# Another order of the last additions, roots and scalings on VectorE and ScalarE behind the last product of a two-layer trunk

## The chip, the cores and the metric

The kernel runs on one core of a Trainium2 chip. The metric is the device time of one execution, in microseconds (us). The work is split over TensorE (PE, matrix products; PEld, its weight loads), VectorE (DVE), ScalarE (ACT), GpSimd (POOL) and the DMA queues, of which SyncE's (SP) matters here. Each engine carries out its own instructions in a fixed order and waits where an operand or a buffer is not ready.

## The reference, cut to what matters

Two layers over x of 512 rows and 1024 columns, all in float32:

```python
for l in range(DEPTH):                       # DEPTH = 2
    x = x + attention_and_output_projection(rmsnorm(x, attn_norm[l]))
    h = rmsnorm(x, mlp_norm[l])
    u = jnp.square(jax.nn.relu(h @ w_ff1[l]))        # 1024 -> 4096
    x = x + u @ w_ff2[l]                             # 4096 -> 1024
return rmsnorm(x, final_norm)
# rmsnorm(x, g) = x * rsqrt(mean(x * x, axis=-1) + 1e-6) * g
```

The change touches only the last lines: the end of the last `u @ w_ff2[l]`, its addition to x, and the final `rmsnorm`.

## The kernel before, in words

A float32 product is made of three products of rounded parts (`three`, L294 to L299: high by high, high by low, low by high). `W` (class `_Weights`) splits each block of weights into those parts: the high part by ScalarE (L115), the low part by VectorE (L131).

The second MLP product is done in four groups `g`. In each, 2x2 blocks of the operands are combined into seven products, called forms, in the order `FORMS2`: "11", "x3", "21", "x2", "x1", "x4", "22". Their sums are held in PSUM banks: chain X for "11", "x2", "x1"; chain V for "x3", "x4"; chain Y for "21"; Z for the very last form. Every chain has two banks, r = 0 and 1.

The output y lies in SBUF as eight pieces of 128 rows by 512 columns, `place(tb, j)`: row block tb = 0 to 3 and column half j = 0, 1. `gather` (L1076) adds the two banks of a chain, times a per-row factor `r2`, to the pieces (2a, j) and (2a + 1, j): one VectorE instruction each (L1084, out<-in reads y<-X, y<-V, y<-Y or y<-Z). In the last group of the last layer the pieces become whole in this order: (2, 0) and (3, 0) after form "21"; (0, 1) and (1, 1) after "x1"; (0, 0) and (1, 0) after "x4" (the list `came`; bank V0 is finished before V1, L1208); (2, 1) and (3, 1) after "22". For "22" the X banks are gathered first (at L1198, into (2, 1) and (3, 1)), and the product itself is put into new banks: Z0 for all 512 columns of (2, 1), then the first 256 columns of (3, 1) in Z1, then its other 256 columns in a bank called `half` (L1201, L1202). `half` takes over the bank of V0. A product of zeros opens it (L1203), and ScalarE then writes the sum so far of those columns into it (`seed`, L1205), so that the last product ends with the whole value in the bank.

The final norm goes row block by row block:

- `square` (L1107, ScalarE): the sum of squares of one piece, into a column of `fin`. It is two instructions, the square and the read of its accumulator.
- `root` (L1136): VectorE adds the two sums (L1138), GpSimd raises the result to the power -1/2 (L1140).
- `weigh` (L1143, VectorE): one piece times the final gain.
- `store` (L1147): one piece times the root, on ScalarE if the piece was weighed before (L1151), otherwise on VectorE with the gain in the same instruction (L1153), and the piece's DMA to the output.
- `last_row` (L1110): for row block 3, the addition of Z1's 256 columns (L1114, `add`), the squares of the two last parts (L1116, `ends`), the addition of the first three sums (L1119, `part`), that of the last one (L1121, `whole`), and the power (L1122).
- `store_last` (L1125): ScalarE scales (3, 0), VectorE the last two parts of 256 columns (L1130), each with its DMA (L1133).

The order of instructions on an engine is chosen by the framework's scheduler when the kernel is built. `behind(a, b)` adds to that only that a stands behind b, without a wait, and `in_order` (L1158) chains a list of steps in this way. At the end there are two such lists, `first` for VectorE (L1259) and `squares` for ScalarE (L1260).

Of the kernel before, what the change touches and what calls it, by code (L numbers as in the profile page):

```python
# [13 lines left out]
ALU = mybir.AluOpType  # L14
# [149 lines left out]
def trunk(ctx, tc, opened, xT, w, w2, w1, gfin, lamv, cos, sin, out):  # L164
    nc = tc.nc
# [167 lines left out]
    for l in range(L):  # L333
        with ExitStack() as actx:
# [113 lines left out]
            ends = {}  # L448
# [387 lines left out]
        with ExitStack() as fctx:  # L836
# [236 lines left out]
            def place(tb, j):  # L1073
                return y[(tb // 2, j)][:, tb % 2, :]
# [31 lines left out]
            def square(tb, j):  # L1106
                return nc.scalar.activation(  # L1107
                    ft(f"junk{tb}{j}"), place(tb, j), AF.Square, accum_out=fin[:, 4 * tb + 4 + j : 4 * tb + 5 + j])

            def last_row(banks_):  # L1110
                half = [place(3, 1)[:, 0:256], banks_[1][:, 0:256]]
                m = [fin[:, n : n + 1] for n in (16, 17, 18, 19, 0)]
                by = r2[:, 3:4]
                add = nc.vector.scalar_tensor_tensor(  # L1114
                    out=half[0], in0=banks_[0][:, 0:256], scalar=by, in1=half[0], op0=ALU.mult, op1=ALU.add)
                ends = [nc.scalar.activation(  # L1116
                    ft(f"junk3{n}")[:, 0:256], half[n], AF.Square, scale=by if n else 1.0,
                    accum_out=m[4] if n else m[1]) for n in range(2)]
                part = nc.vector.tensor_scalar(  # L1119
                    out=m[2], in0=m[0], scalar1=m[1], scalar2=D * EPS, op0=ALU.add, op1=ALU.add)  # L1120
                whole = nc.vector.tensor_tensor(out=m[4], in0=m[4], in1=m[2], op=ALU.add)  # L1121
                nc.gpsimd.tensor_tensor(out=m[3], in0=m[4], in1=mhalf[:, 0:1], op=ALU.pow)  # L1122
                return add, ends, part, whole

            def store_last(bank_):  # L1125
                o = place(3, 1)
# [31 lines left out]
            def in_order(*steps):  # L1158
                for p, q in zip(steps[1:], steps):
                    behind(p, q)  # L1160
# [7 lines left out]
            for g in range(GROUPS):  # L1168
                end = g == GROUPS - 1
                turn[0] = 0  # L1170
                if g:
                    p_, q_, r_, s_ = r_, s_, p_, q_
                    quad_group(g, 0, (p_, q_, r_))
                    quad_group(g, 1, (s_, r_, q_))
                    rest_of_forms(1, "21")
                else:
                    for k in range(2 * GP):
                        for n, pt in enumerate(block(f"f{l}_{g}_{k}", "any")):
                            if (k, n) == (1, 0):
                                rms_square(ssq, f"m{l}")  # L1180
                        evict_whole(pt, k)
                        h_form(k)
                        if last and k > 3:
                            for tb in (2 * (k % 2), 2 * (k % 2) + 1):
                                forth(tb, 1 - k // 6)
                    p_, q_, r_, s_ = ring[0] % 3, 3, (ring[0] + 1) % 3, (ring[0] + 2) % 3
                    held_on = {"Y": [bank("t", f"Y{l}{r}") for r in range(2)], "V": [bank("mm", f"V{l}{r}") for r in range(2)]}
                chains = {"X": [temp(k, f"X{l}{g}{k}") for k in (p_, q_)], **held_on}
                for form in FORMS2:
                    total, to = SUMS[form], chains[CHAIN[form]]  # L1190
                    opens = form == "11" or g == 0 and form in ("x3", "21")
                    if form == "x4" and not end:
                        to = [temp(k, f"W{l}{g}{k}") for k in (r_, s_)]
                        opens = True
                    work = [(c, i, r, 0) for c in range(GP // 2) for i in range(2) for r in range(2)]
                    tail = end and form == "22"
                    if tail and last:
                        gather(total, to)  # L1198
                        to = [temp(k, f"Z{l}{k}") for k in (r_, s_)]
                        opens = True  # L1200
                        work = [(c, i, r, n) for r, n in ((0, 0), (1, 1), (1, 2)) for c in range(GP // 2) for i in range(2)]  # L1201
                        halves = [to[1], bank("mm", "half")]  # L1202
                        nc.tensor.matmul(  # L1203
                            halves[1][:, 0:256], zeros[:, 0:128], zeros[:, 128:384], start=True, stop=False)
                        seed = nc.scalar.activation(  # L1205
                            halves[1][:, 0:256], place(3, 1)[:, 256:512], AF.Copy, scale=mean[:, 3:4])
                    elif end and last and form == "x4":
                        work.sort(key=lambda e: e[2])  # L1208
                    held = {}
                    for n, (c, i, r, part) in enumerate(work):  # L1210
                        if c not in held:
                            held[c] = W.next("f")
                        u = held[c]
                        hi, lo = (e[:, :, i, :] for e in sides[c])
                        rs = slice(r * P, r * P + P)
                        mine = [m for m, e in enumerate(work) if e[2:] == (r, part)]
                        pt, b_ = to[r], wpair(u, i, 512)
                        if part:
                            pt = halves[part - 1][:, 0:256]
                            b_ = [e[:, 256 * part - 256 : 256 * part] for e in b_]  # L1220
                        three(pt, (hi[:, SIDE[form], rs], lo[:, SIDE[form], rs]), b_,
                              opens and n == mine[0] and part < 2, n == mine[-1], not opens)
                        if tail and last and n == 3:
                            squares.append(square(0, 0))
                            first += [root(0), store(0, 0, False), came[1]]
                            squares += [seed, store(0, 1, True), square(1, 0)]
                            first += [root(1), store(1, 0, False), *gather(total, to, (0,))]
                            squares += [store(1, 1, True), square(2, 1)]
                            first.append(root(2))
                        if end and not last and form == "22" and n % 2:  # L1230
                            h = back(n // 2)
                            rests.append(h[1])
                            halfway = h
                    if tail:
                        break
                    if end or form not in ("x3", "21"):
                        came = gather(total, to)
                    if g and form in ("11", "x3"):
                        rest_of_forms(1, "x2" if form == "11" else "22")
                    if end and not last and form in ("21", "x2"):  # L1240
                        for c in range(4 * (form == "x2"), 4 * (form == "x2") + 4):
                            nc.sync.dma_start(x[:, c, :], park[c])
                    if end and last and form == "x3":
                        for c in range(2):
                            nc.sync.dma_start(gf[c], gfin[512 * c : 512 * c + 512].partition_broadcast(P))
                    if end and last and form == "x2":
                        in_order(
                            W.last[0], nc.scalar.activation(gf[0], gf[0], AF.Copy, scale=math.sqrt(D)),
                            nc.scalar.activation(gf[1], gf[1], AF.Copy, scale=-math.sqrt(D)),
                            nc.scalar.activation(x[:, 0, 0:256], gf[1][:, 256:512], AF.Copy, scale=r2[:, 3:4]))  # L1250
                    if end and last and form == "x1":
                        done = ((2, 0), (3, 0), (0, 1), (1, 1))
                        squares = [square(*e) for e in done]
                        weighed = [weigh(*e) for e in done]
                    elif end and last and form == "x4":
                        first = [came[0]]
            if last:
                add_, ends, piece, whole = last_row(halves)
                in_order(*first, add_, piece, store(2, 1, False), whole)  # L1259
                in_order(*squares, *ends, store(2, 0, True), store_last(halves[1]))  # L1260
            else:
                W.pools.pop()
# [88 lines left out]
```

## Time and profile before

| | us |
|---|---|
| median of 3 runs | 1132.72 (1131.89 to 1132.99) |
| the profiled execution, its own time | 1134.11 |
| its span, from the first to the last instruction | 1132.2 |
| PE busy, of the span | 1119.7 |
| DVE, ACT, POOL busy | 915.6, 687.8, 137.6 |
| last product ends, from the span's start | 1123.09 |
| last VectorE instruction ends | 1128.49 |

Times inside the profile count from the span's start. A timeline row gives start, duration, engine, line and operation, the tile written and the tiles read with their shapes, the number of merged instructions, and in square brackets the idle time ahead of it with the instruction that ended it. Instructions of one engine overlap a little: the next one starts before the one ahead is written out. "Pitch" below is the distance from one start to the next when nothing is waited for.

### The profile page before, as it was taken

The numbers are of one execution on the slowest core, as the hardware profiler recorded it, in microseconds if no ns is written. First come the engines' busy times: TensorE is split into PE (matmuls) and PEld (weight loads), VectorE is DVE, ScalarE is ACT, GpSimd is POOL, SyncE is SP. The second block draws the span as 40 slices with busy tenths as digits, with TensorE's granted clock in tenths as the row PEclk, the third lists the DMA queues.
The fourth block names the chain that finished last, engine by engine and source line by source line (L and its number), as shares of the span: only waits on it lengthen the run. The fifth ranks groups of instructions, "written<-read, shape, count | busy, mean of one in ns | idle before, by whom it ended". The sixth has DMA issues, their size and how long they took to land.

```text
span 1132.2 us, 17656 instructions
## 1 busy us (share of the span) xinstructions
PE 1119.7 (99%) x6613; PEld 990.9 (88%) x6613; DVE 915.6 (81%) x1329; ACT 687.8 (61%) x1115; POOL 137.6 (12%) x221
## 2 busy tenths in 40 slices
PE   9999999999999999999999999999999999999996
PEld 7899889888899899898888998988888998998985
DVE  7898788789669779788788877887877797797796
ACT  6456666577558457476355566765774583674664
POOL 1001343101001001001000013330010010010010
PEclk9999999999999999999999999999999999999998
DMA  7665353266876657738227644522487676567362
GB/s 254 153 180 150 93 169 111 70 206 167 228 203 164 170 172 168 197 109 219 90 75 195 178 114 144 154 66 77 153 208 183 190 168 188 142 155 205 94 136 88
DMA packets 59317, 174.99 MB, mean 155 GB/s; under 512 B 7264, under 2 KB 8544, under 8 KB 59232
## 3 DMA queue, kind: packets, MB, share of 16 engines
q1 hardware_dynamic: 50160, 141.84, 40.2%
q0 software_dynamic: 8640, 31.46, 15.7%
q8 instruction: 52, 0.85, 0.3%
q10 hardware_dynamic: 432, 0.56, 0.1%
q14 instruction: 33, 0.27, 0.1%
HBM read 144.47 MB, written 4.19 MB: 131 GB/s over the span
## 4 chain that ended last, share of the span: by engine, by line
PE 94%; DVE 2%; DMA 1%; issue 1%; ACT 1%; POOL 0%; POOLq 0%; DVEq 0%; ACTq 0%
PE X L297 9%; PE X L298 9%; PE X L299 9%; PE V L297 3%; PE V L299 3%; PE V L298 3%; PE wo L297 3%; PE wo L299 3%; PE wo L298 3%; PE f L297 3%; PE f L299 3%; PE f L298 3%; PE Y L297 2%; PE Y L299 2%; PE Y L298 2%; DMA first_b<-in_w 1%
## 5 line engine op out<-in xcount | busy, mean ns | idle before, releaser
L115 ACT ACTIVATE whi<-q 128x1024 fp32r<-128x1024 f32 x96 | 101.5, 1058 | 105.1 <-PE X L299 38.0
L131 DVE TENSOR_TENSOR wlo<-q,whi 128x1024 fp32r<-128x1024 f32 x96 | 116.9, 1220 | 42.1 <-ACT whi L115 38.8
L115 ACT ACTIVATE whi<-raw 128x1024 fp32r<-128x1024 f32 (+1 forms) x82 | 80.8, 993 | 50.2 <-issue 20.3
L131 DVE TENSOR_TENSOR wlo<-raw,whi 128x1024 fp32r<-128x1024 f32 (+1 forms) x82 | 95.2, 1168 | 11.0 <-ACT whi L115 9.2
L297 PE MATMUL X<-whi,Ah 128*128 128x512 f32 x248 | 97.6, 394 | 0.0
L298 PE MATMUL X<-wlo,Ah 128*128 128x512 f32 x248 | 96.7, 390 | 0.0
L299 PE MATMUL X<-whi,Al 128*128 128x512 f32 x248 | 96.6, 390 | 0.0
L131 DVE TENSOR_TENSOR wlo<-waves,whi 128x1024 fp32r<-128x1024 f32 x40 | 48.8, 1221 | 16.9 <-ACT whi L115 16.7
L115 ACT ACTIVATE whi<-waves 128x1024 fp32r<-128x1024 f32 x40 | 42.2, 1056 | 29.7 <-PE X L299 14.9
L297 PEld LDWEIGHTS X<-whi,Ah 128*128 128x128 f32 x248 | 46.6, 188 | 11.9 <-DVE y L1084 1.9
L297 PE MATMUL X<-hxh,whi 128*128 128x256 f32 x192 | 54.7, 285 | 1.9 <-DVE x L1041 1.9
L299 PEld LDWEIGHTS X<-whi,Al 128*128 128x128 f32 x248 | 46.5, 188 | 9.9
L298 PEld LDWEIGHTS X<-wlo,Ah 128*128 128x128 f32 x248 | 46.6, 188 | 8.9
L299 PE MATMUL X<-h_hi,wlo 128*128 128x256 f32 x192 | 54.3, 283 | 0.0
L299 PE MATMUL X<-hxh,wlo 128*128 128x256 f32 x192 | 54.3, 283 | 0.0
L298 PE MATMUL X<-h_lo,whi 128*128 128x256 f32 x192 | 54.3, 283 | 0.0
L298 PE MATMUL X<-hxl,whi 128*128 128x256 f32 x192 | 54.3, 283 | 0.0
L297 PE MATMUL X<-h_hi,whi 128*128 128x256 f32 x192 | 54.3, 283 | 0.0
L297 PE MATMUL f<-h_hi,whi 128*128 128x512 f32 x128 | 50.3, 393 | 0.0
L299 PE MATMUL f<-h_hi,wlo 128*128 128x512 f32 x128 | 49.9, 390 | 0.0
L298 PE MATMUL f<-h_lo,whi 128*128 128x512 f32 x128 | 49.8, 389 | 0.0
L863 POOL DMA_DIRECT2D q<-in_w x32 | 28.5, 890 | 171.2 <-DVE wlo L131 171.2
(740 smaller groups left out, 3817.3 us busy)
## 6 DMA issues: line engine op xcount, KB each, us to landing
raw<-in_w SPq DMA_DIRECT2D x78, 512.0 KB, 3.8
q<-in_w SPq DMA_DIRECT2D x48, 512.0 KB, 4.6
q<-in_w POOLq DMA_DIRECT2D x48, 512.0 KB, 7.3
waves<-in_w SPq DMA_DIRECT2D x28, 512.0 KB, 5.1
first_a<-in_w SPq DMA_DIRECT2D x12, 512.0 KB, 4.7
first_b<-in_w SPq DMA_DIRECT2D x12, 512.0 KB, 5.0
first_c<-in_w SPq DMA_DIRECT2D x12, 512.0 KB, 3.7
norms<-in_w SPq DMA_DIRECT2D x12, 512.0 KB, 3.7
```

The costliest lines, as they stand in the source:

```text
L115: return self.nc.scalar.activation(o, src, AF.Copy)
L131: self.last = h, nc.vector.tensor_tensor(out=lo[:, a:b], in0=raw[:, a:b], in1=hi[:, a:b].bitcast(F32), op=ALU.subtract)
L297: nc.tensor.matmul(pt, ah, bh, start=first, stop=False, skip_group_check=goes_on)
L298: nc.tensor.matmul(pt, ah, bl, start=False, stop=False, skip_group_check=goes_on)
L299: nc.tensor.matmul(pt, al, bh, start=False, stop=last, skip_group_check=goes_on)
L863: nc.gpsimd.dma_start(t, quad(g, q, c), accum_op=ALU.add)
```

## The change

Nothing is computed otherwise, no instruction is added or taken away; the two lists have another order. On VectorE before: came[0] (0, 0), root(0), store(0, 0), came[1] (1, 0), root(1), store(1, 0), gather of Z0 into (2, 1), root(2), add, part, store(2, 1), whole. The gather of X1 into (3, 1), `turned[1]`, and the weighings of (0, 1) and (1, 1), `weighed[2]` and `weighed[3]`, were in no list. After: came[0], weighed[2], turned[1], came[1], root(0), weighed[3], store(0, 0), root(1), gather of Z0, store(1, 0), add (now `add_half`, a function of its own), root(2), part, store(2, 1), whole.

On ScalarE before, behind the squares of (2, 0), (3, 0), (0, 1), (1, 1): square(0, 0), seed, store(0, 1), square(1, 0), store(1, 1), square(2, 1), then the two last squares, store(2, 0) and store(3, 0). After: square(1, 0) stands ahead of store(0, 1); the rest is as it was.

```diff
-            def last_row(banks_):
-                half = [place(3, 1)[:, 0:256], banks_[1][:, 0:256]]
+            def add_half(bank_):
+                o = place(3, 1)[:, 0:256]
+                return nc.vector.scalar_tensor_tensor(
+                    out=o, in0=bank_[:, 0:256], scalar=r2[:, 3:4], in1=o, op0=ALU.mult, op1=ALU.add)
+
+            def last_row(bank_):
+                half = [place(3, 1)[:, 0:256], bank_[:, 0:256]]
                 m = [fin[:, n : n + 1] for n in (16, 17, 18, 19, 0)]
                 by = r2[:, 3:4]
-                add = nc.vector.scalar_tensor_tensor(
-                    out=half[0], in0=banks_[0][:, 0:256], scalar=by, in1=half[0], op0=ALU.mult, op1=ALU.add)
...
-                return add, ends, part, whole
+                return ends, part, whole
...
                     if tail and last:
-                        gather(total, to)
+                        turned = gather(total, to)
...
                         if tail and last and n == 3:
-                            squares.append(square(0, 0))
-                            first += [root(0), store(0, 0, False), came[1]]
-                            squares += [seed, store(0, 1, True), square(1, 0)]
-                            first += [root(1), store(1, 0, False), *gather(total, to, (0,))]
+                            squares += [square(0, 0), seed, square(1, 0)]
+                            first += [weighed[2], turned[1], came[1], root(0), weighed[3], store(0, 0, False)]
+                            squares.append(store(0, 1, True))
+                            first += [root(1), *gather(total, to, (0,)), store(1, 0, False)]
                             squares += [store(1, 1, True), square(2, 1)]
-                            first.append(root(2))
...
             if last:
-                add_, ends, piece, whole = last_row(halves)
-                in_order(*first, add_, piece, store(2, 1, False), whole)
+                first += [add_half(halves[0]), root(2)]
+                ends, piece, whole = last_row(halves[1])
+                in_order(*first, piece, store(2, 1, False), whole)
                 in_order(*squares, *ends, store(2, 0, True), store_last(halves[1]))
```

## The prediction

> **What bounds the kernel now.** The page says that almost the whole chain that ended last is TensorE:
>
> ```profile
> span 1132.2 us, 17656 instructions
> ...
> PE 94%; DVE 2%; DMA 1%; issue 1%; ACT 1%; POOL 0%; POOLq 0%; DVEq 0%; ACTq 0%
> ```
>
> The change leaves the products alone, so only what lies behind them can move. I read the TensorE rows of the last stage next, for when each bank is finished:
>
> ```profile
> 1117.88 0.28 PE L1203 MATMUL half<-edge 128*128 128x256 bf16 x1
> ...
> 1119.83 0.39 PE L299 MATMUL Z<-whi,Al 128*128 128x512 f32 x1
> ...
> 1121.37 0.28 PE L299 MATMUL Z<-whi,Al 128*128 128x256 f32 x1
> ...
> 1122.81 0.28 PE L299 MATMUL half<-whi,Al 128*128 128x256 f32 x1
> ```
>
> ```profile
> L299 PE MATMUL V<-whi,Al x8: 389/389/393, 1106.9 to 1117.0; 128*128 128x512 f32 x8
> ```
>
> V1 is finished at 1117.0 + 0.39 = 1117.4, Z0 at 1119.83 + 0.39 = 1120.22, Z1's half at 1121.37 + 0.28 = 1121.65, and the last product at 1122.81 + 0.28 = 1123.09. From there to the end of the span lie 9.1 us without a product. VectorE's timeline shows who fills them:
>
> ```profile
> 1114.59 1.21 DVE L131 TENSOR_TENSOR wlo<-waves,whi 128x1024 fp32r<-128x1024 f32 x1
> 1115.72 1.28 DVE L1145 TENSOR_TENSOR y<-y,x 128x512 f32<-128x512 f32 x2
> 1116.92 0.74 DVE L1084 SCALAR_TENSOR_TENSOR y<-V,r,y 128x512 f32<-128x512 f32 x1
> 1117.59 0.74 DVE L1084 SCALAR_TENSOR_TENSOR y<-X,r,y 128x512 f32<-128x512 f32 x1
> 1118.46 0.21 DVE L1138 TENSOR_SCALAR fin<-fin 128x1 f32<-128x1 f32 x1
> 1119.36 0.75 DVE L1153 SCALAR_TENSOR_TENSOR y<-y,fin,x 128x512 f32<-128x512 f32 x1 [0.69 <-POOL fin L1140]
> 1120.03 0.75 DVE L1084 SCALAR_TENSOR_TENSOR y<-V,r,y 128x512 f32<-128x512 f32 x1
> 1121.62 0.21 DVE L1138 TENSOR_SCALAR fin<-fin 128x1 f32<-128x1 f32 x1 [0.85 <-ACT x L1107]
> 1122.51 0.75 DVE L1153 SCALAR_TENSOR_TENSOR y<-y,fin,x 128x512 f32<-128x512 f32 x1 [0.67 <-POOL fin L1140]
> 1123.17 0.75 DVE L1084 SCALAR_TENSOR_TENSOR y<-Z,r,y 128x512 f32<-128x512 f32 x1
> 1124.77 0.21 DVE L1138 TENSOR_SCALAR fin<-fin 128x1 f32<-128x1 f32 x1 [0.85 <-ACT x L1107]
> 1124.90 0.47 DVE L1114 SCALAR_TENSOR_TENSOR y<-Z,r,y 128x256 f32<-128x256 f32 x1
> 1126.01 0.21 DVE L1119 TENSOR_SCALAR fin<-fin 128x1 f32<-128x1 f32 x1 [0.64 <-ACT x L1116]
> 1126.14 0.74 DVE L1153 SCALAR_TENSOR_TENSOR y<-y,fin,x 128x512 f32<-128x512 f32 x1
> 1126.80 0.15 DVE L1121 TENSOR_TENSOR fin<-fin 128x1 f32<-128x1 f32 x1
> ```
>
> The same loop runs three times: a gather, a wait for ScalarE's square (0.85), the root's addition, a wait for GpSimd's power (0.67), a store. V1 lies finished from 1117.4 and is fetched at 1120.03; Z0 lies finished from 1120.22 and is fetched at 1123.17. So the tail is bound by three serial chains through ACT, DVE and POOL whose waits nothing fills, and not by the last product. `whole` at 1126.80, the last addition of row block 3, is the point that I follow: behind it come the power, the last scalings and the last DMA, none of which the change touches.
>
> ScalarE and the queue of the stores:
>
> ```profile
> 1120.87 0.63 ACT L1107 ACTIVATE x<-y 128x512 f32<-128x512 f32 x1 [0.78 <-DVE y L1084]
> ...
> 1125.88 0.46 ACT L1116 ACTIVATE x<-half,r 128x256 f32<-128x256 f32 x1
> 1126.24 0.19 ACT L1116 ACTIVATION_READ_ACCUMULATOR x<-half,r 128x1 f32 x1
> 1126.33 0.71 ACT L1151 ACTIVATE y<-y,fin 128x512 f32<-128x512 f32 x1
> ```
>
> ```profile
> 1126.91 0.81 SPq L1155 DMA_DIRECT2D out_xT<-y  x2
> ```
>
> **The change part by part.** No instruction comes or goes. I lay the new order out with steps from these rows. VectorE's pitch is 0.67 for a gather or store (1116.92 to 1117.59), 0.60 for a weighing (two from 1115.72 to 1116.92), 0.13 for a root's addition (1124.77 to 1124.90), 0.40 for the half-wide addition (0.47 less the usual overlap of 0.07). A square leads to its root's addition in 0.75 (1120.87 to 1121.62), a root's addition to the store behind its power in 0.89 (1121.62 to 1122.51).
>
> Up to the last split (L131, 1114.59) nothing moves. At 1115.72 came[0] now takes the place of the weighings: V0's twelve products are sorted ahead of V1's twelve, half-wide products follow each other at 0.12 (twelve from 1121.37 to 1122.81), so wide ones at 0.24, and V1's reach back from 1117.0 to about 1114.4: V0 was done before 1115. Then weighed[2] 1116.39, turned[1] 1116.99, came[1] 1117.66 (V1 is done at 1117.4), root(0) 1118.33, weighed[3] 1118.46. ScalarE squares (0, 0) from about 1116.5 and (1, 0) from about 1118.7: came[1] ends at 1118.40, and the seed ahead of it, whose bank L1203 opens by 1118.16, takes the pitch of a half-wide step, 0.45 (1125.88 to 1126.33). Root(1) can have its sums from 1119.4.
>
> Root(0)'s power is started 0.30 behind root(0), at 1118.63 (before: 1125.06 behind 1124.77), and here the new order has a price: weighed[3], with two operands in SBUF, is already running on VectorE. Rows from the attention show what that does to GpSimd:
>
> ```profile
> 131.48 0.41 POOL L549 TENSOR_TENSOR sig0s<-sig0s,C0s 128x128 f32<-128x128 f32 x1 [0.30 <-DVE C0s L546]
> ...
> 170.57 0.69 POOL L549 TENSOR_TENSOR sig0s<-sig0s,C0s 128x128 f32<-128x128 f32 x1 [1.43 <-DVE C0s L546]
> ```
>
> ```profile
> 170.32 0.66 DVE L238 TENSOR_TENSOR hl0s3q<-t0s3k,hl0s3q 128x512 fp32r<-128x512 f32 x1
> ```
>
> The same GpSimd instruction takes 0.41 alone and 0.69 when started inside a VectorE instruction with two SBUF operands: it ends at 171.26, 0.28 behind VectorE's end at 170.98, so all but its first 0.13 waited. Beside an addition that reads PSUM there is no such delay:
>
> ```profile
> 1125.06 0.54 POOL L1140 TENSOR_TENSOR fin<-fin,mhalf 128x1 f32<-128x1 f32 x1 [2.59 <-DVE fin L1138]
> ```
>
> It ran while L1114 was at work from 1124.90. Weighed[3] (1.28 less a pitch, 0.68) ends at 1119.14, 0.51 behind the power's start, so the power is late by 0.51 - 0.13 = 0.38. Store(0, 0) comes at 1118.33 + 0.89 + 0.38 = 1119.60, root(1) 1120.27, the gather of Z0 1120.40 (Z0 is done at 1120.22). Root(1)'s power runs beside that gather, which reads PSUM, undelayed: store(1, 0) at 1120.27 + 0.89 = 1121.16, add_half at 1121.83 (Z1's half is done at 1121.65), done by 1122.23.
>
> On ScalarE store(1, 1) starts with the same power, 1121.16. Square(2, 1) follows at the pitch of such a store. No row has one directly followed by another; its duration 0.71 less the overlap of 0.09 that the read at 1126.24 shows (it ends at 1126.43, the next starts at 1126.33) gives 0.62, with 0.52 and 0.72 as bounds. So square(2, 1) 1121.78, root(2) 1122.54, store(2, 1) 1123.43, `whole` 0.66 later (1126.14 to 1126.80): 1124.09, with those bounds 0.1 each way.
>
> The other way into `whole` is the last product: 1123.09, about 0.05 to ScalarE, and 0.57 through the last square (1125.88 to 1126.43, and 0.02): 1123.71, so 0.38 is left. `part` needs the square of Z1's half, 1.11 behind add_half (1124.90 to 1126.01), at 1122.94: no wait is added.
>
> `whole` moves from 1126.80 to 1124.09, **2.71 us earlier**. Behind it all keeps its distances. The DMA view (1118 to 1133 in 40 slices) says that the last five stores run as one stretch at about 400 GB/s:
>
> ```profile
> GB/s 0 0 0 0 0 0 0 22 382 410 399 186 0 0 0 0 295 399 399 306 0 0 0 0 0 5 388 415 393 380 407 410 363 36 0 0 0 0 0 0
> ```
>
> It is opened by store(2, 1) (issue 1126.91), which moves by the same 2.71. Stores (1, 0) and (1, 1), 0.5 MB, take 1.3 us there and now start 2.3 us ahead of it, so they stay out of it. Store(2, 0) is issued 0.3 nearer to the end, still behind store(2, 1) in the stretch: nothing, or 0.2 if the queue turns the two round. What hides the moved VectorE work is TensorE, busy to 1123.09; without that cover the three waits of 0.67 to 0.85 come back.
>
> Sum: span 1132.2 - 2.7 = 1129.5, the profiled execution 1134.11 - 2.7 = 1131.4, and for the runs, 1.4 shorter than the profiled one, 1132.72 - 2.7 = **1130.0 us**. The weakest term is the power's delay. With none, every step comes 0.38 earlier until the last product holds `whole` at 1123.71: 3.1 us, 1129.6.
>
> The Trainium skill, SBUF — State Buffer, section "Who interferes with whom", makes that delay a rule: a VectorE instruction with two SBUF inputs and a GpSimd instruction that reads SBUF exclude each other, and the later one blocks fully. Read strictly, with the 115 ns that the page adds behind VectorE's end, the power would be 0.25 later than in my sum; the rows above, with 0.28 behind the end for a job of 0.41, speak for the smaller price.
>
> **The rivals.** (a) The power is blocked for its whole length and begins only behind weighed[3]: `whole` 1124.34, a gain of 2.5, 1130.3. (b) It is not blocked at all, 1129.6; the delayed row speaks against it, though a 128x1 power is a smaller job than that row's.
>
> (c) A late seed. Square(1, 0) now stands behind the seed, which waits for the zero product L1203, and ahead of store(0, 1). From a seed later than 1119.1, root(1) waits for it. Were L1203 queued behind the last Z product, the seed would start at 1121.8, square(1, 0) at 1122.25, root(1) 1123.0, store(1, 1) 1123.9, square(2, 1) 1124.5, root(2) 1125.25, `whole` 1126.8: no gain, 1132.7. Against it: L1203 needs V0's bank free, ran at 1117.88 right behind came[0]'s end at 1117.66, and came[0] is now earlier. If it is queued too early instead, behind V0's last product, TensorE stands 1.8 us until came[0] ends at 1116.46; then the last product ends at 1124.85 and `whole` is at 1125.5: 1131.4.
>
> (d) Slower: TensorE starves behind the list. If the scheduler puts the last split (L131, 1.21) not ahead of the list but behind root(1), at 1120.40, Z's eighth product, which needs it at 1119.83 - 4 x 0.24 = 1118.9, waits until 1121.6. That is 2.7 us, the last product ends at 1125.8, `whole` is at 1126.4: no change. It turns at a stall of 3.1 us (`whole` at 1126.80). Beyond that stands the clock, granted at 0.94 in this stretch and 0.50 in the next:
>
> ```profile
> 1126.00:1126.50 0.50, 0.00 (x0) 0.00 (x0) 0.49 (x2) 0.50 (x3) 0.00 (x0) 0.94 0.00 0
> ```
>
> It fell at 1126.44, 3.35 us behind the last product. A stall of that length puts the 4 wide and 24 half-wide products left (1.0 + 2.9 us) at half speed: the last product ends at 1130.3, `whole` is at 1130.9: 1136.8. Against it: the split's row stands directly behind work that does not move.
>
> **How the numbers follow.** The forecast has 0.55, (a) 0.08, (b) 0.14, (c) 0.17, half of it at each of its times, (d) 0.06. About 0.2%, 2.3 us, is what a measurement of this kernel can tell from no change. The forecast clears it by 0.4 only, and the runs of before spread over 1.1, so I count seven eighths of it, all of (b), half of (a) and a little of (c) as faster: 0.68; the rest but (d) as the same: 0.26; slower 0.06. The range goes from (b) less 0.5 for the spread, 1129.1, to 1131.6, which takes in (a), the bounds of ScalarE's pitch and the milder half of (c).
>
> **What would show it.** In the new profile: y<-V twice between 1115.7 and 1118.4; the first root at 1118.3 and its power stretched from 0.56 to about 0.93; y<-Z at 1120.4, before the products end; `whole` near 1124.1; the last product still at 1123.1. I am wrong if the last product moves, if the seed starts after 1119.1, or if the stores no longer keep their distances behind `whole`.

## The result, and the profile after

| | before | after |
|---|---|---|
| median of 22 runs each, us | 1133.05 (1131.89 to 1136.36) | 1130.57 (1128.77 to 1133.89) |
| ratio after to before, 95% interval | | 0.9977 (0.9971 to 0.9983) |
| the profiled execution: own time, span | 1134.11, 1132.2 | 1130.03, 1127.9 |
| V1 finished to last product's end | 5.73 | 5.73 |
| last product's end to `whole` | 3.71 | 0.92 |
| `whole` to the end of the span | 5.40 | 5.43 |

The change makes the kernel 0.23% faster (0.17 to 0.29%), 2.6 us (the two medians differ by 2.5). The lower three rows are from the two profiles, and all that changed stands in one of them: `whole` has moved 2.79 us towards the last product. The spans differ by 4.3 us. The other 1.5 us lie ahead of the last product, which ends at 1123.09 in the one execution and at 1121.55 in the other. The change doesn't edit that part, and most of the 1.5 us is there long before the tail: the power of L278 in layer 1, in the two profiles of before and after, already stands 1.3 us apart. What made these two executions differ there, no run shows.

```profile
583.64 1.03 POOL L278 TENSOR_TENSOR rcol<-ms,mhalf 128x4 f32<-128x4 f32 x1 [13.02 <-DVE ms L274]
```

```profile
582.31 1.03 POOL L278 TENSOR_TENSOR rcol<-ms,mhalf 128x4 f32<-128x4 f32 x1 [13.00 <-DVE ms L274]
```

In the experiments below whose products stand in the order of after, the last product ends anywhere from 1122.33 to 1124.18. So a span tells little here. Distances between two instructions of the tail repeat to a few hundredths, and they are what I compare. The span itself is given to 0.1 us only, so a distance that ends at its end is no better than that. Where nothing else is said, times below are distances from the last product's end.

VectorE's timeline after. (Line numbers are those of the code of after: L1141 is `root`, L1148 `weigh`, L1156 `store`, L1112 `add_half`, L1122 `part`, L1124 `whole`.)

```profile
1114.17 0.74 DVE L1084 SCALAR_TENSOR_TENSOR y<-V,r,y 128x512 f32<-128x512 f32 x1
1114.84 0.68 DVE L1148 TENSOR_TENSOR y<-y,x 128x512 f32<-128x512 f32 x1
1115.43 0.74 DVE L1084 SCALAR_TENSOR_TENSOR y<-X,r,y 128x512 f32<-128x512 f32 x1
1116.10 0.74 DVE L1084 SCALAR_TENSOR_TENSOR y<-V,r,y 128x512 f32<-128x512 f32 x1
1116.76 0.20 DVE L1141 TENSOR_SCALAR fin<-fin 128x1 f32<-128x1 f32 x1
1116.88 0.68 DVE L1148 TENSOR_TENSOR y<-y,x 128x512 f32<-128x512 f32 x1
1118.02 0.75 DVE L1156 SCALAR_TENSOR_TENSOR y<-y,fin,x 128x512 f32<-128x512 f32 x1 [0.47 <-POOL fin L1143]
1118.69 0.21 DVE L1141 TENSOR_SCALAR fin<-fin 128x1 f32<-128x1 f32 x1
1118.81 0.74 DVE L1084 SCALAR_TENSOR_TENSOR y<-Z,r,y 128x512 f32<-128x512 f32 x1
1119.57 0.75 DVE L1156 SCALAR_TENSOR_TENSOR y<-y,fin,x 128x512 f32<-128x512 f32 x1
1120.24 0.48 DVE L1112 SCALAR_TENSOR_TENSOR y<-Z,r,y 128x256 f32<-128x256 f32 x1
1120.94 0.21 DVE L1141 TENSOR_SCALAR fin<-fin 128x1 f32<-128x1 f32 x1 [0.22 <-ACT x L1107]
1121.35 0.21 DVE L1122 TENSOR_SCALAR fin<-fin 128x1 f32<-128x1 f32 x1 [0.20 <-ACT x L1119]
1121.81 0.75 DVE L1156 SCALAR_TENSOR_TENSOR y<-y,fin,x 128x512 f32<-128x512 f32 x1 [0.24 <-POOL fin L1143]
1122.47 0.15 DVE L1124 TENSOR_TENSOR fin<-fin 128x1 f32<-128x1 f32 x1
```

The brackets are the thing to read. Before, VectorE waited 0.69, 0.85, 0.67, 0.85 and 0.64 us for ScalarE and GpSimd; now it waits 0.47, 0.22, 0.20 and 0.24. The squares and powers, but for the first power, take as long as before; other VectorE work now runs beside them. Z0 is fetched 2.74 us ahead of the last product's end, where it was 0.08 behind it.

TensorE: the zero product now stands directly behind V1's products, and the last product is the line on which the distances rest.

```profile
1115.66 0.28 PE L1206 MATMUL half<-edge 128*128 128x256 bf16 x1
...
1121.27 0.28 PE L299 MATMUL half<-whi,Al 128*128 128x256 f32 x1
```

GpSimd's powers: the first one, with weighed[3] (1116.88) running on VectorE, is 0.95 long, the next one 0.56.

```profile
1117.04 0.95 POOL L1143 TENSOR_TENSOR fin<-fin,mhalf 128x1 f32<-128x1 f32 x1 [30.01 <-DVE fin L1141]
1118.98 0.56 POOL L1143 TENSOR_TENSOR fin<-fin,mhalf 128x1 f32<-128x1 f32 x1 [0.99 <-DVE fin L1141]
```

### The profile page after: what moved, and what is told of

The parts are those of the page before. It is cut to its first block, busy times and chain, and to the rows that moved or that the text cites. A ratio compares the mean times of both kernels' runs of the same rounds, so it can differ in the third digit from the quotient of the medians.

```text
span 1127.9 us, 17657 instructions
## 1 busy us (share of the span) xinstructions
PE 1119.0 (99%) x6613; PEld 990.3 (88%) x6613; DVE 915.7 (81%) x1329; ACT 687.7 (61%) x1115; POOL 138.1 (12%) x221
## 4 chain that ended last, share of the span: by engine, by line
PE 92%; DVE 3%; DMA 2%; ACT 1%; issue 1%; POOL 1%; POOLq 0%; DVEq 0%; ACTq 0%
PE X L297 9%; PE X L298 8%; PE X L299 8%; PE V L297 3%; PE V L299 3%; PE V L298 3%; PE wo L297 3%; PE wo L298 3%; PE wo L299 3%; PE f L299 3%; PE f L297 3%; PE f L298 3%; PE Y L299 2%; PE Y L297 2%; PE Y L298 2%; DMA first_b<-in_w 1%
```

## The experiments

The theory is the prediction's: the end follows `whole`, and `whole` is the end of one chain through VectorE, ScalarE and GpSimd, whose steps can be added up. The rivals: one of the two lists alone carries the gain; GpSimd is not held by what I said; the end is set by the bytes of the last stores; the gain hangs on nothing but VectorE. Each kernel was profiled once; the one with root(0) ahead of came[1] was also timed in five rounds. Times are from the last product's end, but for the last column. The two right-hand columns end at the span's end, so a difference of less than 0.1 in them means nothing.

| kernel | `whole` | end of the span | `whole` to the end |
|---|---|---|---|
| before | 3.71 | 9.11 | 5.40 |
| after | 0.92 | 6.35 | 5.43 |
| VectorE's list only | 1.63 | 7.05 | 5.42 |
| ScalarE's list only | 3.71 | 9.07 | 5.36 |
| front half of VectorE's list | 2.32 | 7.72 | 5.40 |
| weighed[3] from PSUM | 0.70 | 6.08 | 5.38 |
| root(0) ahead of came[1] | 0.69 | 6.07 | 5.38 |
| ... and row 2 earlier | 0.80 | 6.15 | 5.35 |
| ... and part behind its store | 0.69 | 6.07 | 5.38 |
| one store less | 0.92 | 6.33 | 5.41 |
| late seed | 2.70 | 8.14 | 5.44 |
| last split behind root(1) | 2.10 | 7.45 | 5.35 |

### VectorE's list only

```diff
-                            squares += [square(0, 0), seed, square(1, 0)]
+                            squares += [square(0, 0), seed]
...
-                            squares.append(store(0, 1, True))
+                            squares += [store(0, 1, True), square(1, 0)]
```

> VectorE has the order of after, ScalarE that of before: square(1, 0) behind store(0, 1) again. Read by the tail: `whole` stood 3.71 us behind the end of the last product before and 0.92 after. Theory (the tail is a chain through VectorE, ScalarE and GpSimd, each step in the order of its engine): store(0, 1) holds ScalarE 0.63 from the first power on, root(1) comes 0.7 later, and everything behind it, so `whole` is 1.6 us behind the last product. Rival (the VectorE order alone carries the gain, ScalarE has room): 0.9 us, as after.

1.63, as the theory had it. On ScalarE store(0, 1), started by the first power, now stands ahead of square(1, 0):

```profile
1119.22 0.72 ACT L1154 ACTIVATE y<-y,fin 128x512 f32<-128x512 f32 x1 [1.27 <-POOL fin L1143]
1119.86 0.61 ACT L1107 ACTIVATE x<-y 128x512 f32<-128x512 f32 x1
```

and VectorE waits 0.62 for it at root(1):

```profile
1120.59 0.21 DVE L1141 TENSOR_SCALAR fin<-fin 128x1 f32<-128x1 f32 x1 [0.62 <-ACT x L1107]
```

ScalarE idled 1.27 us ahead of that store, with the piece (1, 0) ready for most of it.

### ScalarE's list only

```diff
-                            first += [weighed[2], turned[1], came[1], root(0), weighed[3], store(0, 0, False)]
+                            first += [root(0), store(0, 0, False), came[1]]
...
-                            first += [root(1), *gather(total, to, (0,)), store(1, 0, False)]
+                            first += [root(1), store(1, 0, False), *gather(total, to, (0,))]
...
-                first += [add_half(halves[0]), root(2)]
+                first += [root(2), add_half(halves[0])]
```

> ScalarE has the order of after, VectorE that of before, the weighings and the gather of X1 in no list again. Theory: square(1, 0) waits for came[1], which VectorE fetches only behind store(0, 0), so ScalarE's new order brings nothing and store(0, 1) only moves behind that square: `whole` 3.7 us behind the last product, as before. Rival (ScalarE's order is worth 0.7 us by itself): 3.0 us.

3.71, to the hundredth as before. Square(1, 0) stands first and waits 1.97 us for came[1]:

```profile
1120.11 0.63 ACT L1107 ACTIVATE x<-y 128x512 f32<-128x512 f32 x1 [1.97 <-DVE y L1084]
```

So ScalarE's move is worth nothing alone and 0.71 beside VectorE's (1.63 to 0.92). The parts don't add up one by one: each is worth what the other uncovers.

### The front half of VectorE's list

```diff
-                            first += [root(1), *gather(total, to, (0,)), store(1, 0, False)]
+                            first += [root(1), store(1, 0, False), *gather(total, to, (0,))]
...
-                first += [add_half(halves[0]), root(2)]
+                first += [root(2), add_half(halves[0])]
```

> As after up to root(1), ScalarE too; behind it VectorE has the order of before (store(1, 0), gather of Z0, root(2), add, part). Theory: the gather of Z0 waits again for root(1)'s power, 0.9 us, and add for root(2): `whole` 2.2 to 2.3 us behind the last product, so a half of the gain comes from each half of the list. Rival (the gain is all in fetching V1 early): 0.9 to 1.1 us.

2.32: the front half gives 1.39 of the 2.79, the back half 1.40. The waits that come back are these, the power of root(1) and the square of (2, 1), and behind them 0.64 at `part` where after waits 0.20:

```profile
1122.21 0.75 DVE L1156 SCALAR_TENSOR_TENSOR y<-y,fin,x 128x512 f32<-128x512 f32 x1 [0.67 <-POOL fin L1143]
1122.87 0.74 DVE L1084 SCALAR_TENSOR_TENSOR y<-Z,r,y 128x512 f32<-128x512 f32 x1
1124.47 0.21 DVE L1141 TENSOR_SCALAR fin<-fin 128x1 f32<-128x1 f32 x1 [0.85 <-ACT x L1107]
```

### What held the first power

```diff
+                            weighed[3] = nc.vector.tensor_mul(place(1, 1), chains["V"][1], gf[1])
                             first += [weighed[2], turned[1], came[1], root(0), weighed[3], store(0, 0, False)]
...
-                        weighed = [weigh(*e) for e in done]
+                        weighed = [weigh(*e) for e in done[:3]] + [None]
```

> weighed[3] multiplies the gain with the PSUM bank V1 in place of the piece (1, 1) in SBUF, so that one piece of the output is another; the number, order and widths of the instructions are those of after. Theory (GpSimd is kept waiting by a VectorE instruction with two SBUF operands): the first power takes 0.56 in place of 0.95 us, store(0, 0) comes 0.4 earlier and `whole` is 0.7 us behind the last product, held by the last square. Rival (any VectorE work beside the power, or the first power itself, makes it long): 0.95 and 0.92 us as after.

The weighing stands at the same place and is as long, and the power beside it takes 0.57:

```profile
1117.75 0.68 DVE L1228 TENSOR_TENSOR y<-V,x 128x512 f32<-128x512 f32 x1
```

```profile
1117.92 0.57 POOL L1143 TENSOR_TENSOR fin<-fin,mhalf 128x1 f32<-128x1 f32 x1 [30.01 <-DVE fin L1141]
```

One operand in PSUM in place of SBUF is all that differs, so the 0.38 us were the price of the second SBUF operand, and neither of VectorE being busy nor of the first power. `whole` came to 0.70, no lower: behind this the last square holds it.

### Root(0) ahead of came[1]

The same price avoided with the right result: the gather, which reads PSUM, runs beside the power, and the weighing behind it.

```diff
-                            first += [weighed[2], turned[1], came[1], root(0), weighed[3], store(0, 0, False)]
+                            first += [weighed[2], turned[1], root(0), came[1], weighed[3], store(0, 0, False)]
```

> root(0) stands ahead of came[1], all else as after: the gather of V1, which reads PSUM, runs beside the first power, and weighed[3] starts at the power's end. Theory (the power was held by weighed[3]'s SBUF operands, and behind that only the last square holds `whole`): the first power takes 0.56, `whole` is 0.7 us behind the last product (0.92 after, 3.71 before), and the tail from the last product's end to the end of the span, 6.35 after, is 6.1 us; against before 0.26% faster, which the spread of the runs can hardly tell from after. Rival (GpSimd is held by any VectorE instruction): 0.95, 0.92 and 6.35 us.

```profile
1118.77 0.57 POOL L1143 TENSOR_TENSOR fin<-fin,mhalf 128x1 f32<-128x1 f32 x1 [29.33 <-DVE fin L1141]
```

`whole` is at 0.69, 0.23 earlier than after, and the tail is 6.07 against 6.35. Against before the ratio is 0.9973 (0.9963 to 0.9982), a median of 1130.63 against 1133.63 on that chip. The interval overlaps that of after widely: the profile shows this order to be the better one, and the runs can't.

### Row 2 earlier

On top of the last kernel, square(2, 1) ahead of store(1, 1) and root(2) ahead of add_half:

```diff
-                            squares += [store(1, 1, True), square(2, 1)]
+                            ahead_ = store(1, 1, True)
+                            squares += [square(2, 1), ahead_]
...
-                first += [add_half(halves[0]), root(2)]
+                first.append(root(2))
+                first.append(add_half(halves[0]))
```

> As the kernel with root(0) ahead of came[1], and besides square(2, 1) ahead of store(1, 1) on ScalarE and root(2) ahead of add_half on VectorE. Store(2, 1), which opens the last stretch of stores, starts at 0.4 us ahead of the last product's end (0.26 behind it after); `whole` stays at 0.7 behind it. Theory (the end follows `whole`, its three last stores and their landing): a tail of 6.1 us. Rival (the stretch of 1.05 MB at 400 GB/s sets the end from its opening): 5.7 to 5.8 us.

This expectation missed: store(2, 1) starts 0.14 behind the last product's end and not 0.4 ahead of it, and `whole` is at 0.80 and not at 0.7. I had overlooked that `part` stands ahead of it in the list and waits for the square of Z1's half, which moving root(2) up had made later:

```profile
1122.66 0.21 DVE L1122 TENSOR_SCALAR fin<-fin 128x1 f32<-128x1 f32 x1 [0.64 <-ACT x L1119]
1122.79 0.74 DVE L1156 SCALAR_TENSOR_TENSOR y<-y,fin,x 128x512 f32<-128x512 f32 x1
1123.45 0.15 DVE L1124 TENSOR_TENSOR fin<-fin 128x1 f32<-128x1 f32 x1
```

With `part` behind the store:

```diff
-                in_order(*first, piece, store(2, 1, False), whole)
+                in_order(*first, store(2, 1, False), piece, whole)
```

> As the kernel with row 2 earlier, with part now behind store(2, 1) on VectorE: there part, which waits for the square of Z1's half, held store(2, 1) at 0.14 behind the last product. Theory: store(2, 1) starts 0.4 ahead of the last product's end, `whole` is back at 0.7 behind it, held by the last square alone, and the tail is 6.1 us as with root(0) moved only: an earlier store of row 2 buys nothing. Rival (the opening of the last stretch of stores counts): a tail of 5.7 us or less.

```profile
1122.07 0.75 DVE L1156 SCALAR_TENSOR_TENSOR y<-y,fin,x 128x512 f32<-128x512 f32 x1 [0.26 <-POOL fin L1143]
1122.73 0.21 DVE L1122 TENSOR_SCALAR fin<-fin 128x1 f32<-128x1 f32 x1
1123.12 0.16 DVE L1124 TENSOR_TENSOR fin<-fin 128x1 f32<-128x1 f32 x1 [0.18 <-ACT x L1119]
```

Store(2, 1) now starts 0.36 ahead of the last product's end (1122.43), `whole` waits only for ScalarE's last square, and the tail is 6.07, as without the two moves. With only root(0) moved, store(2, 1) starts 0.14 ahead of the last product's end (1123.79 against 1123.93). Opening the last stretch of stores 0.2 us earlier than there bought nothing.

### One store less

```diff
-                (nc.scalar if (tb, j) == (3, 0) else nc.sync).dma_start(out[tb, :, 512 * j : 512 * j + 512], o)
+                if (tb, j) != (2, 0):
+                    (nc.scalar if (tb, j) == (3, 0) else nc.sync).dma_start(out[tb, :, 512 * j : 512 * j + 512], o)
```

> As after without the DMA of store(2, 0): 256 KB of the output are not written. Theory (the end follows `whole` and the three stores behind it): `whole` at 0.92, the tail 6.2 to 6.35 us, since the queue ahead of the last stores is shorter by no more than it is late. Rival (the last stretch of stores sets the end by its bytes): 0.64 us less (256 KB at 400 GB/s), 5.7 us.

The tail is 6.33 against 6.35, which is the same as far as the spans can tell; the rival's 0.64 us less is ruled out. The DMA view of each kernel's last 8 us, in 40 slices of 0.2, shows why; after:

```profile
GB/s 379 440 369 440 379 62 266 420 389 410 379 440 307 10 0 0 0 113 430 389 430 379 440 379 359 405 394 440 369 384 312 21 0 0 0 0 0 0 0 0
```

One store less:

```profile
GB/s 369 389 420 389 430 113 225 410 410 379 430 389 359 21 0 0 0 92 430 389 369 31 0 51 348 435 384 440 359 374 231 0 0 0 0 0 0 0 0 0
```

The missing store leaves a gap of a few slices, and the last three stores, which wait for the last power, fill the rest at the same full rate from their own start on. Their last bytes come earlier by a slice of 0.2 at most, and the span, read to 0.1, shows no earlier end.

### A late seed

```diff
-                        nc.tensor.matmul(
+                        zero = nc.tensor.matmul(
                             halves[1][:, 0:256], zeros[:, 0:128], zeros[:, 128:384], start=True, stop=False)
...
+                        if tail and last and n == 7:
+                            behind(zero, ended)
```

(`ended` is the last product of Z1.)

> The zero product that opens the bank `half` is queued behind the last Z product, all else as after: the prediction's rival (c). Theory (square(1, 0), and with it root(1), hangs on the seed): the last product ends 0.8 us later against the start of came[0], which is 8.2 us instead of 7.4 ahead of it, and `whole` stands 2.7 to 2.8 us behind it: the gain of after is gone or nearly so. Rival (the seed has slack on ScalarE): only the last product moves, `whole` 0.9 us behind it.

As the theory had it: the seed waits 4.46 us for its bank, square(1, 0) stands behind it, and root(1) waits 2.51 for that.

```profile
1121.33 0.48 ACT L1208 ACTIVATE half<-y,mean 128x256 f32<-128x256 f32 x1 [4.46 <-PE half L1206]
```

```profile
1122.48 0.21 DVE L1141 TENSOR_SCALAR fin<-fin 128x1 f32<-128x1 f32 x1 [2.51 <-ACT x L1107]
```

`whole` at 2.70 behind a last product that itself ends 0.82 later (6.55 behind V1, 5.73 after). From V1's end to `whole` it is 9.25 us, where before has 9.44 and after 6.65: the gain of 2.79 is gone but for 0.19.

### The last split behind root(1)

```diff
+                            behind(W.rest_of[_INDEX[("f", l, g, "22", 1)]], first[7])
```

> The last split of weights (L131) stands behind root(1) on VectorE, all else as after: the prediction's rival (d). The scheduler has put the products that do not need it in between (all of the first weight block for Z1 and `half`), so TensorE waits for 0.8 us and not for 2.7. Theory (once TensorE no longer covers the moved work, the gain goes): the last product ends 0.8 us later against the end of V, Z0 is fetched 2.4 us later than after, `whole` is 2.1 us behind the last product, 0.8 us of the gain of 2.8 are left, and the granted clock stays at 1.00 up to the last product, since the wait is far from 3.3 us. Rival (the split is off the path): `whole` 0.9 us behind the last product.

TensorE works off what doesn't need the split, then stands for 0.8 us:

```profile
1120.41 0.28 PE L297 MATMUL half<-whi,Ah 128*128 128x256 f32 x1
1121.34 0.50 PE L298 MATMUL Z<-wlo,Ah 128*128 128x512 f32 x1 [0.64 <-DVE wlo L131]
```

(From 1120.53, a product pitch of 0.12 behind the first row, to 1121.34.) The granted clock, the third figure from the right in each row of the stretches before, in and behind the wait, is 1.00 throughout:

```profile
1119.80:1120.60 0.80, 0.80 (x8) 0.69 (x6) 0.80 (x3) 0.20 (x1) 0.37 (x1) 1.00 0.00 0
1120.60:1121.30 0.70, 0.09 (x1) 0.00 (x0) 0.68 (x1) 0.00 (x0) 0.70 (x1) 1.00 0.63 243
1121.30:1123.90 2.60, 2.56 (x15) 2.19 (x15) 1.10 (x2) 0.98 (x2) 0.40 (x1) 1.00 0.59 227
```

`whole` is 2.10 behind the last product, which itself ends 6.65 behind V1's end where after has 5.73. From V1's end to `whole` it is 8.75: 0.69 of the gain of 2.79 are left. The wait of TensorE is only part of this. The products that filled the gap were put ahead of Z0's last five, so Z0 is finished later, and VectorE waits for it:

```profile
1122.80 0.75 DVE L1084 SCALAR_TENSOR_TENSOR y<-Z,r,y 128x512 f32<-128x512 f32 x1 [1.52 <-PE Z L299]
```

This gather stands 1.15 ahead of the last product's end, where after has 2.74, and the squares, roots and stores of row blocks 2 and 3 follow it. So the moved work needs products to run under, and their order counts as well: of the 2.10 by which `whole` is later behind V1 than in after, 0.92 are the later last product, and the rest is the late Z0.

## Why the prediction was right, step by step

Told from the start of came[0], 1115.72 in the prediction and 1114.17 in the profile of after:

| step | predicted | measured |
|---|---|---|
| root(0) | 2.61 | 2.59 |
| length of its power | 0.94 | 0.95 |
| store(0, 0) | 3.88 | 3.85 |
| gather of Z0 | 4.68 | 4.64 |
| store(1, 0) | 5.44 | 5.40 |
| add_half | 6.11 | 6.07 |
| root(2) | 6.82 | 6.77 |
| store(2, 1) | 7.71 | 7.64 |
| `whole` | 8.37 | 8.30 |
| last product's end | 7.37 | 7.38 |

**What bounds.** The reading that three serial chains fill the tail, with work at hand to put into their waits, holds. The prediction priced the change as a whole; the experiments split it. With ScalarE's list in place, the front half of VectorE's gives 1.39 of the 2.79 and the back half the other 1.40. VectorE's whole list without ScalarE's gives 2.08, and ScalarE's without VectorE's gives nothing.

**The price inside the change.** The power held by weighed[3] was the weakest term, 0.38, and came out at 0.95 - 0.56 = 0.39; taking the second SBUF operand away, by PSUM or by order, takes it away. The Trainium skill, SBUF — State Buffer, section "Who interferes with whom", states that a VectorE instruction with two SBUF inputs contends with a GpSimd instruction that reads SBUF, and that one with at most one SBUF input, outside the 2-port modes, doesn't. The runs agree: 0.95 beside two SBUF operands, 0.57 beside one. Why the two engines contend, no run here shows. The strict reading, rival (a), doesn't hold here: the power ended at 1117.99, 0.43 behind weighed[3]'s end (1116.88 + 0.68), although alone it takes 0.56. Of the 0.25 by which (a) is later, 0.12 are the 115 ns, and no run here shows such a term for a power. The Trainium skill, on the same page, states them for a DMA that waits for its descriptors from GpSimd.

**A size that was off.** For the way from the last product to `whole` I had 0.62, and so 0.38 left over; it measures 0.69 to 0.70 where it binds. ScalarE starts the last square 0.09 to 0.10 behind the last product, and not 0.05. Without the hold on the power the gain is therefore 3.0 us (`whole` at 3.71 and at 0.69), and not the 3.1 of rival (b).

**The tail behind `whole`.** The prediction said that it keeps its distances, and it does, 5.35 to 5.44 in all twelve kernels. Its reason, that the stretch of the last five stores is opened by store(2, 1) and moves with it, falls: with 256 KB fewer, or with that store moved against `whole`, the end stays where `whole` puts it. In the change both moved by about the same, so the sum came out all the same: at this step that was luck. What keeps the distances is only that the end follows `whole`; what the 5.4 us behind it consist of was not taken apart.

**The rivals.** (c) is no idle danger: a late seed takes back 2.6 of the 2.8 us. That the scheduler did the opposite and put the zero product ahead of Z, where came[0] frees the bank earlier, was the prediction's argument against it. The other half of (c), a zero product queued too early, was not run. (d) had the wait too long and left out another cost: I had TensorE stand for 2.7 us, and it stood 0.8, since the scheduler fills the gap with other products; but these push back Z0. In the sum (d) left 0.4 of the gain, and the run left 0.7. No run came near the wait of 3.3 us from which I had the clock fall; that part of (d) wasn't tried and stays open.

**The size against the noise.** For `whole` 2.71 us were forecast and 2.79 measured; for the runs 2.7 were forecast and 2.6 (1.9 to 3.3) measured, 1130.57 where the forecast has 1130.0. The executions of one program spread over 4 to 5 us, while the distances of the tail repeat, so most of the spread must come from ahead of the tail. The interval lies clear of no change, but its lower end, 1.9, is below the 2.3 us that the prediction took for the least that can be told from none. By that line the runs leave open whether this counts as faster, to which it gave a chance of 0.68; it is the 2.79 of the profile that shows the gain. The prediction also took a last product that moves from 1123.1 for a sign of being wrong: it ended at 1121.55, but 5.73 behind V1's end as before, so that sign is to be read from V1.

## What to carry to other kernels

At a tail of short chains across engines, lay the steps out one by one with pitches and hand-over times from the trace, and put whatever lies finished into the waits; the order on every engine involved counts, since half a reordering can be worth nothing. Before a GpSimd instruction is started beside VectorE work, see where that work's operands lie: put the one that reads PSUM beside it, and the one with two SBUF operands behind it. A gain of this size is read from distances inside the profile; the runs told it from nothing only with 22 of each, and couldn't tell the better of two orders 0.23 us apart.

## What the runs showed of the hardware that was not expected

The prediction had a hold on GpSimd, worked out from one job of 128x128. Not expected was how closely its length goes with the VectorE instruction even for the smallest job. With the last split (1.22 us long) beside it, a power of one element per partition takes 1.47 in place of 0.56 us, and ends at 1121.70, 0.41 behind the split's end (1120.07 + 1.22). With the shorter weighing it ended 0.43 behind. So in both cases some 0.42 of the job's 0.56 is left at the end of the VectorE instruction. The reading that fits both is that about the first 0.14 passes beside it and the rest waits; the rows show only the two ends.

```profile
1120.07 1.22 DVE L131 TENSOR_TENSOR wlo<-waves,whi 128x1024 fp32r<-128x1024 f32 x1
```

```profile
1120.23 1.47 POOL L1143 TENSOR_TENSOR fin<-fin,mhalf 128x1 f32<-128x1 f32 x1 [0.99 <-DVE fin L1141]
```
